# Row sums over partitions taken once per attention head, and once for the embedding, in place of once per half of the tokens

## The chip, the cores and the metric

The kernel runs on one core of a Trainium2 chip. The metric is device time in microseconds of one execution. A core has five engines that run their own instruction streams and wait for one another by semaphores: TensorE (PE, its weight loads shown apart as PEld), VectorE (DVE), ScalarE (ACT), GpSimd (POOL) and SyncE (SP), which here issues the DMAs. Line numbers, as L116, are those of the kernel before, unless the text says they are of the change.

## The reference

One layer of a hybrid encoder on 1024 tokens of width 1024. The normalised input goes through one projection of eight parts. Four parts feed differential attention (4 heads, two softmax maps each, an RMS norm per head and token, a gate), four a gated short convolution. Both are projected back together, normalised and added to x; an embedding p, projected and normalised per token, is added through a gate.

```python
h = rms_norm(x, pre_norm_gain[i])
proj = h @ w_in[i]
q, k, v, z_a, b_gate, c_gate, u, z_c = jnp.split(proj, N_IN_PARTS, axis=-1)
...
attn = diff_attention(q, k, v, lam, slopes)
attn = rms_norm(attn, subln_gain[i], SUBLN_EPS) * (1.0 - lambda_init)
attn = attn.reshape(bsz, seq, D_ATTN) * jax.nn.silu(z_a)
...
mixed = jnp.concatenate([attn, conv_out], axis=-1) @ w_out[i]
x = x + rms_norm(mixed, post_norm_gain[i])
e = rms_norm(p[i] @ w_ple_proj[i], ple_norm_gain[i])
x = x + jax.nn.sigmoid(x @ w_ple_gate[i]) * e
```

The change concerns two of these norms: the one of each head (`subln_gain`) and the one of the embedding (`ple_norm_gain`). Each needs, for every token, a sum of squares over features.

## The kernel before

Everything is held with features on the 128 partitions and tokens along the free axis, in two halves of 512 tokens (`HALF`). Products run in fp32 split into a high and a low part, so each tile product is three matmuls (`mm3`, L99 to L102) for each of eight slices of the contraction: 24 matmuls of 128x512 for one output tile of one half.

The program first projects the embedding (results go to `e_dram`), loads and scales x, and makes queries, keys and the values of all heads. Then come the four heads. Head h takes the projections of its query and key, and then the steps of its row of `PLAN` (L31 to L36): `a` is the softmax of four blocks of 128 queries (L220 to L254), `v` recalls the values, `z` projects the gate (`ev_z`, L214: the product by R, ACT's tanh at L217, the gate product L218), `g0` and `g1` are the value products of the two halves (`values`, L256), `n0` and `n1` apply the row scales (`scale_values`, L283), `c1` is one tile of the convolution's projections (L433 and around), and `s0`, `s1` are the sums of the embedding's two halves (`embed_scale`, L447). After the heads come the output projection, its norm and the gate.

A sum of squares per token is a sum over partitions. `column_sums` (L105) does it in four steps: DVE transposes 32x32 blocks (L107) and reduces over the 32 (L109), which leaves 128x16; an extra 16 columns (L111) carry a second quantity of the head, the inverse of its softmax sums; and a matmul with the constant matrix `fold` (L116) adds up the four groups of partitions. Its result lies in a PSUM bank of tag "t". There are two such banks, and the transposes of the attention weights (`tpw`, L264) go through the same two; a bank is given out again once the last reader of its former content is done.

In `values` the sum is followed by the row scale: DVE copies the extra columns (`rb`, L276), multiplies twice (L277 reads the bank, L278), scales (L96), POOL raises to the power -1/2 (`pow`, L97, with the constants of `nhalf`), DVE multiplies once more (L280). `scale_values` spreads the result over partitions by a transpose (L120 by L286) and multiplies it into the tile (L287). `embed_scale` reloads eight tiles of `e_dram`, squares them on ACT (L453), adds them on POOL (L455), and makes sum, pow and a factor 0.5 (L456 to L458).

Weight tiles are loaded and split by `load_w` (L122): ACT writes the high part (L89), POOL the low part `w` (L90). The attention weights `wt` are split by ACT (L89) and DVE (L90) after the transposes.

The order in which each engine works is not that of the source line by line. A scheduler places every engine's instructions at build time, by the steps of `PLAN`, the priorities that follow from them and its own model; each engine then runs its list strictly in order. Two or three steps are therefore interleaved: projections of one head fill PE while the softmax of another is under way.

```python
def bank_t(name):
    return ps_s.tile([P, HALF], F32, tag="t", bufs=2, name=name)
...
ms = bank_t("ms")
T.matmul(out=ms[:, :n], lhsT=fold, rhs=part[:, :n], start=True, stop=True)
```

## Time and profile before

| | |
|---|---|
| runs | 642.95, 643.99, 644.54 us; median 643.99 |
| the profiled execution | 643.39 us, of which the span of instructions is 641.6 and 1.8 lies outside |
| mean granted clock of TensorE | 0.996 of full speed |
| busy | PE 632.6 us (99%), DVE 447.9 (70%), ACT 242.3 (38%), POOL 227.6 (35%) |
| HBM | 48.4 MB read, 12.6 MB written, 95 GB/s over the span |

The profile is one execution. The bracket behind a row of a timeline says how long the engine stood idle before that instruction, and what released it. PE's instructions overlap, so the time that one costs is read from start to start. A wait is put down to the last of the semaphores that the instruction waited for.

### The profile page before, as it was taken

How to read it: one execution, taken by the hardware profiler on the slowest of the kernel's cores; microseconds unless marked ns; L12 is line 12 of the kernel's file. 1: busy time of each engine (PE TensorE's matmuls, PEld its weight loads, DVE VectorE, ACT ScalarE, POOL GpSimd, SP SyncE). 2: the span in 40 equal slices, each digit the busy share in tenths (PEclk: the TensorE clock that was granted, in tenths of full speed). 3: DMA queues.
4: the chain of work that ended last, by engine and by line, in shares of the span. 5: the costliest groups of instructions: out<-in, count | busy, mean ns of one | idle time of the engine just before them, and what ended most of it. 6: DMA issues, size and time to landing. Idle time of an engine off the chain costs nothing.

```text
span 641.6 us, 8064 instructions
## 1 busy us (share of the span) xinstructions
PE 632.6 (99%) x2941; PEld 524.8 (82%) x2941; DVE 447.9 (70%) x824; ACT 242.3 (38%) x442; POOL 227.6 (35%) x114
## 2 busy tenths in 40 slices
PE   8999999999999999999999999999999999999997
PEld 4888788888888888887888888888888888888886
DVE  6977612688786688776886999628993179898342
ACT  5936312334454333553343533322732225413111
POOL 2013300324326636237461142433760087741000
PEclk8999999999999999999999999999999999999999
DMA  8976612210244112353113411111360034124231
GB/s 301 391 268 161 228 78 102 88 39 27 83 130 149 50 33 59 85 170 97 36 33 90 127 46 34 42 55 36 119 242 33 2 98 150 64 84 146 84 114 50
DMA packets 35511, 67.78 MB, mean 106 GB/s; under 512 B 3600, under 2 KB 12304, under 8 KB 35472
## 3 DMA queue, kind: packets, MB, share of 16 engines
q1 hardware_dynamic: 35328, 67.14, 31.6%
q8 instruction: 23, 0.38, 0.2%
q10 hardware_dynamic: 144, 0.13, 0.1%
q14 instruction: 16, 0.13, 0.1%
HBM read 48.38 MB, written 12.58 MB: 95 GB/s over the span
## 4 chain that ended last, share of the span: by engine, by line
PE 89%; DVE 4%; DMA 3%; POOL 2%; ACT 1%; issue 1%; POOLq 0%; DVEq 0%; ACTq 0%
PE pj L100 13%; PE pj L102 13%; PE pj L101 13%; PE o L102 9%; PE o L100 9%; PE o L101 9%; PE s L237 5%; PE tpw L264 2%; PE v L100 2%; PE v L102 2%; PE v L101 2%; PE av L102 1%; PE ple L101 1%; PE av L101 1%; POOL mix L455 1%; PE av L100 1%
## 5 line engine op out<-in xcount | busy, mean ns | idle before, releaser
L100 PE MATMUL pj<-hT,w 128*128 128x512 f32 x448 | 176.3, 394 | 0.0
L101 PE MATMUL pj<-hT,w 128*128 128x512 f32 x448 | 176.2, 393 | 0.0
L102 PE MATMUL pj<-hT,w 128*128 128x512 f32 x448 | 176.2, 393 | 0.0
L90 POOL TENSOR_TENSOR w<-raw,w 128x1024 fp32r<-128x1024 f32 x41 | 105.6, 2581 | 145.1 <-ACT w L89 145.1
L102 PEld LDWEIGHTS pj<-hT,w 128*128 128x128 f32 x448 | 84.2, 188 | 16.4
L101 PEld LDWEIGHTS pj<-hT,w 128*128 128x128 f32 x448 | 84.2, 188 | 16.2
L100 PEld LDWEIGHTS pj<-hT,w 128*128 128x128 f32 x448 | 84.2, 188 | 16.1
L245 ACT ACTIVATE p<-p,nm 128x128 f32<-128x128 f32 (+7 forms) x64 | 49.4, 772 | 70.6 <-DVE nm L241 60.7
L89 ACT CAST w<-raw 128x1024 fp32r<-128x1024 f32 x44 | 45.8, 1047 | 19.4 <-issue 11.0
L102 PE MATMUL o<-x,w 128*128 128x512 f32 (+1 forms) x136 | 51.3, 377 | 0.0
L100 PE MATMUL o<-x,w 128*128 128x512 f32 (+1 forms) x136 | 51.2, 377 | 0.0
L101 PE MATMUL o<-x,w 128*128 128x512 f32 (+1 forms) x136 | 51.2, 377 | 0.0
L100 PE MATMUL o<-mT,w 128*128 128x512 f32 x128 | 49.8, 389 | 0.0
L101 PE MATMUL o<-mT,w 128*128 128x512 f32 x128 | 49.8, 389 | 0.0
L102 PE MATMUL o<-mT,w 128*128 128x512 f32 x128 | 49.7, 390 | 0.0
L237 PE MATMUL s<-ks,qs 128*128 128x512 f32 (+2 forms) x192 | 47.5, 346 | 0.5 <-ACT w L89 0.5
L89 ACT CAST wt<-tpw 128x512 fp32r<-128x512 f32 (+3 forms) x48 | 21.1, 479 | 60.2 <-PE tpw L264 60.2
L90 DVE TENSOR_TENSOR wt<-tpw,wt 128x512 fp32r<-128x512 f32 (+3 forms) x48 | 25.3, 550 | 26.3 <-ACT wt L89 26.2
L241 DVE CUSTOM_DVE_ANT_0 p<-s,bias 128x512 f32<-128x512 f32 (+3 forms) x64 | 34.8, 564 | 9.4 <-PE s L237 5.4
L237 PEld LDWEIGHTS s<-ks,qs 128*128 128x128 f32 x192 | 33.3, 188 | 5.8 <-ACT w L89 0.8
L418 POOL TENSOR_TENSOR mix<-mix,R 128x512 f32<-128x512 f32 x8 | 12.3, 1542 | 66.1 <-DVE mix L417 64.0
L253 DVE SCALAR_TENSOR_TENSOR p<-p,rl,p 128x128 f32<-128x128 f32 (+7 forms) x32 | 32.7, 1021 | 0.4
(142 smaller groups left out, 1101.6 us busy)
## 6 DMA issues: line engine op xcount, KB each, us to landing
raw<-in_w_in SPq DMA_DIRECT2D x32, 512.0 KB, 3.4
mix<-in_xT SPq DMA_DIRECT2D x16, 256.0 KB, 5.5
e_dram<-e SPq DMA_DIRECT2D x16, 256.0 KB, 6.0
mix<-e_dram SPq DMA_DIRECT2D x16, 256.0 KB, 3.0
ks<-ks SPq DMA_DIRECT2D x16, 256.0 KB, 3.6
v_dram<-v SPq DMA_DIRECT2D x8, 512.0 KB, 2.6
vs<-v_dram SPq DMA_DIRECT2D x32, 128.0 KB, 2.7
raw<-in_w_out SPq DMA_DIRECT2D x8, 512.0 KB, 3.3
```

Source lines behind the costliest of these rows:

```text
L89: A.copy(out=hi, in_=src)
L90: (lo_eng or V).tensor_tensor(out=lo, in0=src, in1=hi.bitcast(F32), op=sub)
L100: T.matmul(out=ps, lhsT=ah, rhs=bh, start=first, stop=False)
L101: T.matmul(out=ps, lhsT=ah, rhs=bl, start=False, stop=False)
L102: T.matmul(out=ps, lhsT=al, rhs=bh, start=False, stop=last)
L237: T.matmul(out=banks[m][:, :nn], lhsT=s.qs[:, m, qi], rhs=s.ks[:, m, part, c], start=part == 0, stop=part == 1)
L241: V.tensor_tensor_reduce(out=pr[m][:, c0:c0 + n], in0=banks[m][:, :n], in1=s.bias[:, b0:b0 + n], scale=-1.0, scalar=low[m], op0=add, op1=A ...
L245: A.activation(out=pr[m][:, :W], in_=pr[m][:, :W], func=AF.Exp, scale=-1.0, bias=low[m], accum_out=l[:, m:m + 1])
L253: V.scalar_tensor_tensor(out=pr[0][:, :W], in0=pr[1][:, :W], scalar=rl, in1=pr[0][:, :W], op0=mult, op1=add)
L264: T.transpose(out=tp[:, ii * P:(ii + 1) * P], in_=s.ws[ii][:, j * P:(j + 1) * P], identity=ident)
L418: G.tensor_tensor(out=o, in0=o, in1=R[n], op=mult)
L455: G.tensor_tensor(out=acc, in0=acc, in1=e, op=add)
```

## The change

The sum over partitions is cut in two functions. `partial` makes the reduction of one half into a given slice; `total` runs the matmul with `fold` over whatever width it is handed. In a head, `g0` and `g1` now only leave their reductions and extra columns in one tile of 64 columns (`part4`), and a new step `r`, `row_scales`, placed in `PLAN` after `g1` and a `c1` and ahead of `n0`, does one sum of 64 columns, then the products, the pow and the last product over 32 columns for both halves (lines 285 to 289 of the change, with L96 and L97 for the scale and the pow). The embedding's first half, in head 0, only leaves its reduction in `rs_e`; the second half, in head 1, does one sum, one pow and one factor 0.5 of 32 columns. The sums of x's norm and of the norm behind the output projection stay one per half; some small tiles are made wider so that addresses stay aligned, and `nhalf` has 32 columns.

The steps of `PLAN` change as shown for one head; the other three rows are changed in the same manner (`r` in all, `s` in the first two).

```
-    ['a0123', 'z', 'v', 'g0', 'a4567', 'g1', 'c1', 'n0', 'c1', 's1', 'n1', 'c1'],
+    ['a0123', 'z', 'v', 'g0', 'a4567', 'g1', 'c1', 'r', 'n0', 'c1', 's', 'n1', 'c1'],
```

```diff
-    small_c = edge.tile([P, 96], F32, name="small_c")
+    small_c = edge.tile([P, 224], F32, name="small_c")
...
-    nhalf = small_c[:, 4:20]
+    nhalf = small_c[:, 93:125]
...
-    def column_sums(acc, pool, extra=None, tag="flip"):
+    def partial(part, acc, pool, tag="flip"):
         flip = pool.tile([P, HALF], F32, tag=tag, name="flip")
         V.transpose(out=flip, in_=acc)
-        part = tiny.tile([P, 32], F32, tag="part", name="part")
-        V.tensor_reduce(out=part[:, 0:16], in_=flip.rearrange("p (f r) -> p f r", r=32), axis=AX.X, op=add)
-        if extra is not None:
-            V.tensor_tensor(out=part[:, 16:32].rearrange("p (t f) -> p t f", t=4),
-                            in0=extra.unsqueeze(2).broadcast_to([P, 4, 4]),
-                            in1=own.unsqueeze(1).broadcast_to([P, 4, 4]), op=mult)
-        n = 16 if extra is None else 32
-        ms = bank_t("ms")
-        T.matmul(out=ms[:, :n], lhsT=fold, rhs=part[:, :n], start=True, stop=True)
+        V.tensor_reduce(out=part, in_=flip.rearrange("p (f r) -> p f r", r=32), axis=AX.X, op=add)
+
+    def total(part):
+        ms = bank_t("ms")[:, :part.shape[-1]]
+        T.matmul(out=ms, lhsT=fold, rhs=part, start=True, stop=True)
         return ms
+
+    def column_sums(acc, pool, tag="flip"):
+        part = tiny.tile([P, 16], F32, tag="part", name="part")
+        partial(part, acc, pool, tag)
+        return total(part)
...
-    r_col = const.tile([P, NT + 80], F32, name="r_col")[:, :NT]
+    r_col = const.tile([P, NT + 96], F32, name="r_col")[:, :NT]
...
-                s.rs = {}
...
-                ms = column_sums(sq, ap, extra=r0)
-                rb = tiny.tile([P, 16], F32, tag="rb", name="rb")
-                rs = tiny.tile([P, 16], F32, tag="rs", name="rs")
-                V.tensor_copy(out=rb, in_=ms[:, 16:32])
-                V.tensor_tensor(out=rs, in0=ms[:, 0:16], in1=rb, op=mult)
+                if g == 0:
+                    s.part = tiny.tile([P, 64], F32, tag="part4", name="part4")
+                c = slice(16 * g, 16 * g + 16)
+                partial(s.part[:, c], sq, ap)
+                V.tensor_tensor(out=s.part[:, 32 + 16 * g:48 + 16 * g].rearrange("p (t f) -> p t f", t=4),
+                                in0=r0.unsqueeze(2).broadcast_to([P, 4, 4]),
+                                in1=own.unsqueeze(1).broadcast_to([P, 4, 4]), op=mult)
+
+            def row_scales(s):
+                ms = total(s.part)
+                rb = tiny.tile([P, 32], F32, tag="rb", name="rb")
+                rs = tiny.tile([P, 32], F32, tag="rs", name="rs")
+                V.tensor_copy(out=rb, in_=ms[:, 32:64])
+                V.tensor_tensor(out=rs, in0=ms[:, 0:32], in1=rb, op=mult)
                 V.tensor_tensor(out=rs, in0=rs, in1=rb, op=mult)
                 rsqrt(rs, rs, P, 1e-5)
                 V.tensor_tensor(out=rs, in0=rs, in1=rb, op=mult)
-                s.rs[g] = rs
+                s.rs = [rs[:, 0:16], rs[:, 16:32]]
...
-                r = tiny.tile([P, 16], F32, tag="rs", name="rsx")
-                rsqrt(r, column_sums(sums_x(n), rowp, tag="t")[:, :16], D, 1e-6)
+                r = tiny.tile([P, 32], F32, tag="rs", name="rsx")[:, :16]
+                rsqrt(r, column_sums(sums_x(n), rowp, tag="t"), D, 1e-6)
...
-            r = rs_e[:, 16 * n:16 * n + 16]
-            rsqrt(r, column_sums(acc, ap)[:, :16], D, 1e-6)
-            V.tensor_scalar(out=r, in0=r, scalar1=0.5, scalar2=None, op0=mult)
+            partial(rs_e[:, 16 * n:16 * n + 16], acc, ap)
+            if n:
+                rsqrt(rs_e, total(rs_e), D, 1e-6)
+                V.tensor_scalar(out=rs_e, in0=rs_e, scalar1=0.5, scalar2=None, op0=mult)
...
+                elif k == "r":
+                    hd.row_scales()
                 elif k == "s":
                     with tc.issue_after(hd.last.ins):
-                        embed_scale(int(v))
+                        embed_scale(h)
...
-            r = tiny.tile([P, 16], F32, tag="rs", name="rso")
-            rsqrt(r, column_sums(accs[n], cp)[:, :16], D, 1e-6)
+            r = tiny.tile([P, 32], F32, tag="rs", name="rso")[:, :16]
+            rsqrt(r, column_sums(accs[n], cp), D, 1e-6)
```

What each engine runs, and in which order, moves with it. Three places follow, as the two kernels' programs have them.

PE, head 0's sum. Before, at the sum of the second half (`ms`, and `pj` a projection, `s` scores of head 1):

```order
L237 MATMUL s_1919<-ks,qs 128x256 x2
L102 MATMUL pj<-hT_0_94,w 128x512
L116 MATMUL ms<-part,fold 128x32
L100 MATMUL pj<-hT_1_95,w 128x512
L101 MATMUL pj<-hT_1_95,w 128x512
```

In the change, at the one sum of the head, and further on, at the first transposes (`tpw`) behind it that need its bank:

```order
L102 MATMUL pj<-hT_0_94,w 128x512
L112 MATMUL ms<-part_1092,fold 128x64
L264 MATMUL tpw<-ident,p_1686 128x128
L264 MATMUL tpw<-ident,p_1706 128x128
L264 MATMUL tpw<-ident,p_1725 128x128
```

```order
L237 MATMUL s_1912<-ks,qs 128x512 x2
L100 MATMUL pj<-hT_7_101,w 128x512
L101 MATMUL pj<-hT_7_101,w 128x512
L264 MATMUL tpw<-ident,p_1706 128x128
L264 MATMUL tpw<-ident,p_1725 128x128
L100 MATMUL av<-wt,vs 128x512
L264 MATMUL tpw<-ident,p_1744 128x128
L237 MATMUL s_1913<-ks,qs 128x512 x2
L101 MATMUL av<-wt,vs 128x512
L102 MATMUL av<-wt,vs 128x512
```

The transposes of head 1's weights now stand right behind the sum. Four of them fill the other "t" bank; 28 instructions behind the sum's own end, the next transposes come back to the sum's bank.

DVE at the same place, from the product of the gate of head 1 (L216) on. Before:

```order
L216 TENSOR_TENSOR mix_1_113<-pj,R_129 128x512
L241 ISA p_1910,nm<-s_1912,bias 128x384
L241 ISA nm 128x1
L276 COPY rb<-ms 128x16
L277 TENSOR_TENSOR rs<-ms,rb 128x16
L218 SCALAR_TENSOR_TENSOR mix_1_113<-tz,mix_1_113 128x512
L278 TENSOR_TENSOR rs<-rs,rb 128x16
L96 TENSOR_SCALAR rs<-rs 128x16
L241 ISA p_1910,nm<-s_1920,bias,nm 128x256
```

In the change:

```order
L216 TENSOR_TENSOR mix_1_113<-pj,R_129 128x512
L241 ISA p_1883,nm<-s_1885,bias 128x384
L241 ISA nm 128x1
L285 COPY rb<-ms 128x32
L241 ISA p_1882,nm<-s_1884,bias 128x384
L241 ISA nm 128x1
L218 SCALAR_TENSOR_TENSOR mix_1_113<-tz,mix_1_113 128x512
L286 TENSOR_TENSOR rs<-ms,rb 128x32
L241 ISA p_1882,nm<-s_1892,bias,nm 128x256
L241 ISA nm 128x1
L287 TENSOR_TENSOR rs<-rs,rb 128x32
L96 TENSOR_SCALAR rs<-rs 128x32
```

The product that reads the sum's bank last (`rs<-ms,rb`) stood ahead of the gate product L218 and stands behind it now, and a split of `wt` and more score reductions (L241) stand behind that.

PE at the embedding's second sum. Before, and then in the change:

```order
L100 MATMUL pj<-hT_3_105,w 128x512
L101 MATMUL pj<-hT_3_105,w 128x512
L116 MATMUL ms<-part,fold 128x16
L264 MATMUL tpw<-ident,p_2491 128x128
```

```order
L102 MATMUL pj<-hT_0_94,w 128x512
L100 MATMUL pj<-hT_1_95,w 128x512
L112 MATMUL ms<-small_c,fold 128x32
L264 MATMUL tpw<-ident,p_2462 128x128
```

The sum went from between the projections of one weight tile to the next one's: between it and the last value product of head 1 there are 103 projection matmuls and 14 of the scores before, and 121 and 24 in the change.

## Rows read from the trace of the kernel before

**Rows 1.** The page's part 1, busy us (share) xinstructions of each engine

```profile
PE 632.6 (99%) x2941; PEld 524.8 (82%) x2941; DVE 447.9 (70%) x824; ACT 242.3 (38%) x442; POOL 227.6 (35%) x114
```

**Rows 2.** Stretches: length, busy of PE, PEld, DVE, ACT, POOL; clock, DMA, GB/s

```profile
200.00:300.00 100.00, 100.00 (x481) 83.84 (x480) 73.07 (x162) 42.63 (x81) 52.94 (x29) 1.00 0.28 85
300.00:305.00 5.00, 4.51 (x23) 3.54 (x23) 4.96 (x7) 0.59 (x1) 2.21 (x1) 1.00 0.33 104
305.00:475.00 170.00, 170.00 (x814) 141.98 (x814) 135.12 (x272) 66.26 (x121) 68.49 (x30) 1.00 0.24 78
```

**Rows 3.** What PE waited for: us in total, times, longest

```profile
PE ms L116 <- DVE part L109: 0.5, 1, 0.5
```

**Rows 4.** PE's timeline at head 0's two sums: start, us, instruction [idle <-releaser]

```profile
150.74 0.30 PE L116 MATMUL ms<-part,fold 128*128 128x32 f32 x2
150.88 0.41 PE L264 MATMUL tpw<-ident,p 128*128 128x128 f32 x2
151.05 0.48 PE L102 MATMUL pj<-hT,w 128*128 128x512 f32 x1
...
198.27 0.30 PE L116 MATMUL ms<-part,fold 128*128 128x32 f32 x2
```

**Rows 5.** PE's timeline at the second embedding sum

```profile
301.62 0.39 PE L100 MATMUL pj<-hT,w 128*128 128x512 f32 x1
...
302.53 0.39 PE L101 MATMUL pj<-hT,w 128*128 128x512 f32 x1
303.41 0.40 PE L116 MATMUL ms<-part,fold 128*128 128x16 f32 x2 [0.49 <-DVE part L109]
```

**Rows 6.** The chain of waits, 275 to 310 us: start, us, what

```profile
277.29 0.48 ACT sq L270
...
290.92 2.91 POOL rs L97
...
300.61 2.15 DVE ty L440
302.76 0.61 DVE part L109
```

**Rows 7.** DVE's timeline, 198.5 to 208 us

```profile
198.82 0.17 DVE L277 TENSOR_TENSOR rs<-ms,rb 128x16 f32<-128x16 f32 x1
201.63 2.84 DVE L218 SCALAR_TENSOR_TENSOR mix<-tz,mix 128x512 f32<-128x512 f32 x1 [2.64 <-ACT tz L217]
204.40 0.16 DVE L278 TENSOR_TENSOR rs<-rs,rb 128x16 f32<-128x16 f32 x1
```

**Rows 8.** ACT's timeline, 199 to 206 us

```profile
200.97 0.62 ACT L217 ACTIVATE tz<-mix 128x512 f32<-128x512 f32 x1
...
204.08 0.63 ACT L453 ACTIVATE mix<-mix 128x512 f32<-128x512 f32 x1 [1.07 <-DMA mix<-e_dram]
```

**Rows 9.** POOL's timeline, 198 to 214 us

```profile
201.53 2.39 POOL L90 TENSOR_TENSOR w<-raw,w 128x1024 fp32r<-128x1024 f32 x1
204.85 2.94 POOL L97 TENSOR_TENSOR rs<-rs,small_c 128x16 f32<-128x16 f32 x1 [0.92 <-DVE rs L96]
```

**Rows 10.** Groups of POOL by shape: count | busy, mean ns | idle before

```profile
L97 POOL TENSOR_TENSOR rs<-rs,small_c 128x16 f32<-128x16 f32 x8 | 23.7, 2961 | 16.6 <-DVE rs L96 16.5
...
L455 POOL TENSOR_TENSOR mix<-mix,mix 128x512 f32<-128x512 f32 x14 | 19.1, 1362 | 28.1 <-ACT mix L453 27.8
...
L77 POOL MEMSET small_c<- 128x16 f32 x1 | 0.1, 111 | 0.0
```

**Rows 11.** What DVE waited for

```profile
DVE rs L280 <- POOL rs L97: 6.2, 4, 2.4
```

**Rows 12.** Groups of DVE by shape

```profile
L90 DVE TENSOR_TENSOR wt<-tpw,wt 128x512 fp32r<-128x512 f32 x24 | 15.9, 683 | 21.3 <-ACT wt L89 21.1
...
L241 DVE CUSTOM_DVE_ANT_0 p<-s,bias,nm 128x256 f32<-128x256 f32 x16 | 7.6, 478 | 0.9 <-PE s L237 0.8
```

**Rows 13.** DVE's timeline, 290.9 to 293.9 us

```profile
292.19 0.69 DVE L440 SCALAR_TENSOR_TENSOR ty<-ty,y 128x512 f32<-128x512 f32 x1 [0.36 <-ACT ty L438]
```

6 rows, old and new, of the table PLAN are left out of this document.

## The prediction

> **What bounds the kernel now.** I read first the page's busy shares, then the table by stretches, then the waits of PE, then the timelines at the places that the change touches, and last the groups of POOL and DVE. Busy shares: PE works 632.6 us of the span, DVE 70%, POOL 35% [rows 1], so the time is PE's work plus the few moments in which PE stands. By stretches: PE is busy for the whole of 200 to 300 and of 305 to 475 us at full granted clock, and loses 0.49 us in the five microseconds between [rows 2]. PE's instruction order under the change differs from the order before only between about 147 and 473 us of the trace, so nothing outside that stretch can be won. The waits of PE name a single one in it: a row-sum matmul that waits 0.5 us for DVE's reduction [rows 3]. All that the change takes from DVE and POOL can therefore only matter where PE comes to wait for it.
>
> **The sums on PE.** A sum is two PE instructions. Start to start, the pair takes 150.88 - 150.74 = 0.14 us [rows 4]; nothing hides them, since PE is the bound. The change has 9 sums where there were 14, so 5 x 0.14 = 0.70 us go. Four of those left get 32 columns more, the one of the embedding 16 more. Lower bound of that: nothing. Upper bound: the rate of a wide matmul, 0.227 us for 512 columns (four of them from 301.62 to 302.53 [rows 5]), which is 0.014 us for 32 columns and, two instructions each, 4 x 0.028 + 0.014 = 0.13 us. I take the middle, 0.06. Sum: -0.64 us (-0.70 to -0.57).
>
> **The wait at 303 us.** The second embedding sum starts 303.41 - 302.53 = 0.88 us after the matmul ahead of it where 0.23 is usual [rows 5]: 0.65 us. The chain shows its cause: from the end of head 1's last product (the square at 277.29) through eight reloads, squares and POOL adds to the reduction at 302.76 there are about 26.1 us, one pow of 2.91 us on POOL among them, and a DVE product at 300.61 that took 2.15 us [rows 6]. Between head 1's last value product and this sum PE had 103 projection matmuls and 14 score matmuls, 58,400 columns or 25.8 us; in the order of the change it has 121 and 24, 70,208 columns or 31.1 us. If the pow there becomes twice as long, the chain grows by 2.9 to 29.0 us, still below 31.1. So I take the whole 0.65 us as gained; it stays if other work on POOL is put ahead of the chain. Term: -0.65 us (-0.65 to 0).
>
> **A new wait at 204 us.** Head 0's sum now stands at the place of its second half's sum, 198.1 us (198.27 less one pair [rows 4]). Its result lies in one of the two banks that the transposes of the weights use too. The next four transposes take the other bank; the ones behind them need this one. By the order of the change there lie between: the pair (0.14), four transposes (0.085 each, two in 151.05 - 150.88 [rows 4]), 22 matmuls of 512 columns (4.99) and two of 256 (0.23), so 5.7 us; PE wants the bank at 203.85 us. DVE frees it with its second reader, `rs<-ms,rb`. Before, that ran at 198.82, ahead of the gate product L218; now it stands behind L218. L218 started at 201.63, after 2.64 us of waiting for ACT's tanh, took 2.84 us, and L278 behind it ran at 204.40 [rows 7]; the tanh itself ran at 200.97 on ACT [rows 8]. L218 was that long because POOL split a weight tile from 201.53 for 2.39 us [rows 9]; the like product at 292.19 took 0.69 [rows 13].
>
> So the bank comes free at about 204.4 + 0.17 = 204.6, and PE stands 0.75 us. Behind it DVE still has a score reduction (0.48 and 0.08), L287, L96 (0.17 each, as L277 [rows 7]) and then the weight remainder (0.68 [rows 12]) that the second matmul of the value product needs, about 0.95 us of PE work after the late transpose, at 205.55. DVE is through at 206.05 to 206.1: another 0.5 us. A POOL add behind the square of 204.08 [rows 8] would hold L287 if two-input products are held by adds too, to about 206.05, and the remainder to 206.9: 1.3 instead of 0.5. Bounds: 0, if the weight split no longer falls on L218 (it then ends at 202.3), and 2.1. I take 1.3, since the split, the tanh and L218 stand in the same neighbourhood in both orders.
>
> By the Trainium skill, "SBUF — State Buffer", section Terms, a port pair shared by VectorE and GpSimd is locked for the full instruction and "the loser **fully blocks**"; its contention section includes VectorE operations with two inputs in SBUF. The trace agrees at 201.63, with 2.84 us, and does not agree for the pow, beside which a product took 0.69 us. By the rule alone the new wait would be 2.1 us and the sum +0.8.
>
> **The wider pows.** The head's and the embedding's pows go from ten of 16 columns to five of 32. The price of 32 is in no row. Lower bound: 2.96 us, if columns cost nothing; upper: 5.9, if it is per column. A memset of the same 16 columns took 0.11 us and an add of 512 columns 1.36 [rows 10], so little of 2.96 is fixed, and I take 5.9. POOL's total is then unchanged, and its idle time of 65% [rows 1] takes it. DVE needs the result for the last scale product, L289. The DVE work that the order of the change has between L96 and L289 is, by the groups' means, about 6.5, 5.3, 4.8 and 4.1 us in heads 0 to 3; the shortest is six products of 128x512 at 0.68 [rows 12]. DVE then waits about 0, 0.6, 1.1 and 1.8 us. Before, it waited four times at this place, 2.4 us at the longest [rows 11], and PE waited for none of it [rows 3]. Cost: nothing (0 to 3.5). If that cover went, a late weight remainder or a late transposed bank would be next to hold PE.
>
> **The rest.** Some 22 small DVE operations go, about 0.17 us each [rows 7], 3.7 us of an engine with 30% to spare: nothing, and what they free on DVE is idle time. The embedding's first half no longer asks PE for a sum in head 0, and the factor 0.5 is applied once. DMAs and ACT's instructions are the same in number. The row scales of head 3's first half come later: from their sum to the output projection's first use of that tile the order has about 22 us of PE work, and the pow with the products ahead of and behind it is some 12 by the groups' means: nothing.
>
> **Sum.** -0.64 - 0.65 + 1.3 = 0.0 us. On the profiled execution that is 643.4 us; the median of the three runs lies 0.6 above it (643.99; the runs reach from 642.95 to 644.54), and the forecast on it is 644.0.
>
> **Rivals.** 0.3%, 1.93 us, is about what a measurement of this kernel can tell from no change.
> - *The new wait costs nothing* (0.25). The scheduler's order and the real times part: if the weight split on POOL lands a microsecond or two away, L218 takes 0.7 us and the bank is free before 203.85. Then -1.3 us: 642.7. For it: these 2 us decide all. Against: nothing in the change moves that split. Runs that scatter like those shown put some of this case beyond 0.3%.
> - *The wait at 303 us remains* (0.13). The longer pow or another split ahead of the adds eats the 2.1 us between 29.0 and 31.1. Then 644.6.
> - *Slower: the doubled pow reaches PE* (0.14). DVE runs in order; with L289 waiting, the remainders and reductions behind it wait as well. It decides from the point where the wait exceeds what the place can bear, 2.4 us by [rows 11] in the order before, perhaps less in the new one. With all of 0.6 + 1.1 + 1.8 = 3.5 us on PE: 647.5. For it: four bursts instead of eight are less evenly spread. Against: the longest wait forecast, 1.8, is below 2.4.
> - *Slower: the pow holds DVE as the weight split does* (0.03). Then nothing covers it: each head's DVE stands up to 5.9 us, 3.5 above what was borne, 14 us in four heads: 658. Against it stands the product of 0.69 us at 292.19 [rows 13], inside the pow at 290.92 [rows 6]. This is what the page named above would have, if a pow counts as its GpSimd operation that reads SBUF.
> - That the change does not do what it says is left out: the order has 9 sums and 5 pows fewer.
>
> **How the numbers follow.** The likeliest case, no measurable change at 644.0, has 0.45. Faster by over 0.3% is 0.10, all of it out of the 0.25 at 642.7. Slower is 0.14 + 0.03 = 0.17. The remaining 0.73 lies within 0.3%. The range goes from 642.1, the case at 642.7 with the scatter of the runs, to 646.3, the last rival with two thirds of its price; it leaves out some 0.1 on each side.
>
> **What would show it.** PE with 10 instructions fewer, sums of 64 columns at 0.14 to 0.17 us; no wait of a sum near 303 us; a wait of a transpose on `rs`, and of a value product on `wt`, near 204 us, 1.3 us together; pows of 5.9 us with DVE waits below 2. Wrong it would be with PE idle above 3 us between 147 and 473 us, or with pows of 32 columns near 3 us, or with none of the waits at 204.

## The result and the profile after

| | before | after |
|---|---|---|
| median | 643.47 us (642.71 to 644.67, 6 runs) | 648.99 us (648.06 to 655.21, 6 runs) |
| ratio of the means | | 1.011, 95% interval 1.0087 to 1.0133 |
| the profiled execution | 643.39 us, span 641.6 | 648.06 us, span 645.8 |

The changed kernel is slower, by 5.5 us (0.9%) between the medians and by 1.1% between the means, where no change was forecast (644.0, range 642.1 to 646.3). Two of its six runs took 652.9 and 655.2 us, at a mean granted clock of 0.991 and 0.990, and raise the mean; the other four lie within 1 us of one another at 0.996 or more, and why those two are longer is not shown, since there is no trace of them.

The page's part 1, the table of what PE waited for and the stretches (length, busy of PE, PEld, DVE, ACT and POOL; clock, DMA share, GB/s) answer to [rows 1], [rows 3] and [rows 2]:

```profile
PE 633.0 (98%) x2931; PEld 523.2 (81%) x2931; DVE 441.4 (68%) x802; ACT 242.3 (38%) x442; POOL 223.9 (35%) x109
```

```profile
PE o L100 <- DVE mix L454: 2.5, 1, 2.5
...
PE s L237 <- issue: 1.6, 1, 1.6
...
PE tpw L264 <- DVE rs L286: 0.6, 1, 0.6
PE av L101 <- DVE wt L90: 0.6, 1, 0.6
```

```profile
200.00:300.00 100.00, 97.06 (x462) 80.05 (x460) 73.38 (x161) 41.26 (x80) 53.44 (x27) 1.00 0.30 85
...
475.00:625.00 150.00, 147.57 (x653) 122.27 (x654) 97.25 (x102) 42.78 (x71) 54.84 (x26) 1.00 0.28 96
```

DVE has 22 instructions less and PE 10, as the order had it. But PE, which lost 0.5 us between 150 and 475 us before [rows 2, 3], now loses 2.94 in 200 to 300 and 2.43 behind 475 us. The wait of the embedding's sum is gone; four others and some smaller losses are there instead. The timeline of PE shows the four (start, duration, instruction, idle time before it and its releaser):

```profile
204.03 0.41 PE L264 MATMUL tpw<-ident,p 128*128 128x128 f32 x2 [0.61 <-DVE rs L286]
205.84 0.50 PE L101 MATMUL av<-wt,vs 128*128 128x512 f32 x1 [0.59 <-DVE wt L90]
...
290.91 0.39 PE L100 MATMUL pj<-hT,w 128*128 128x512 f32 x1
292.90 0.47 PE L237 MATMUL s<-ks,qs 128*128 128x256 f32 x2 [1.60 <-issue]
...
474.58 0.39 PE L102 MATMUL o<-mT,w 128*128 128x512 f32 x1
477.43 0.47 PE L100 MATMUL o<-mT,w 128*128 128x512 f32 x1 [2.46 <-DVE mix L454]
```

From start to start against the usual 0.227 us, the last two cost 1.77 (292.90 - 290.91 less 0.227) and 2.62 us (477.43 - 474.58 less 0.227), the first two 0.77 and 0.76; smaller ones at 285.4 and 410.4 us cost 0.31 and 0.16. The sums themselves did what was said; the pair of 64 columns takes 197.52 - 197.35 = 0.17 us:

```profile
197.35 0.33 PE L112 MATMUL ms<-part,fold 128*128 128x64 f32 x2
197.52 0.50 PE L264 MATMUL tpw<-ident,p 128*128 128x128 f32 x3
```

An instruction that both kernels run in the same place behind the heads, the first `rso` scaling, gives the balance. One line for each kernel, before and then after (first and last start behind the durations):

```profile
L96 DVE TENSOR_SCALAR rso<-ms x2: 167/170/173, 513.9 to 558.5; 128x16 f32<-128x16 f32 x2
```

```profile
L96 DVE TENSOR_SCALAR rso<-ms x2: 167/171/175, 518.5 to 563.1; 128x16 f32<-128x16 f32 x2
```

It starts 4.6 us later. The terms: 0.6 gained in the first 75 us, where the order is the same in both and arrivals differ from run to run; 0.6 gained by the sums; 0.65 by the embedding's sum [rows 5]; 1.53 lost at 204 us; 2.08 at 285 and 291 us; 2.78 at 410 and 475 us. Together 4.54 us.

**204 us.** DVE's timeline of after, beside [rows 7]:

```profile
200.94 2.85 DVE L218 SCALAR_TENSOR_TENSOR mix<-tz,mix 128x512 f32<-128x512 f32 x1 [2.54 <-ACT tz L217]
203.71 0.18 DVE L286 TENSOR_TENSOR rs<-ms,rb 128x32 f32<-128x32 f32 x1
...
204.21 0.77 DVE L287 TENSOR_TENSOR rs<-rs,rb 128x32 f32<-128x32 f32 x1
...
205.10 0.68 DVE L90 TENSOR_TENSOR wt<-tpw,wt 128x512 fp32r<-128x512 f32 x1
```

The gate product L218 again started beside a weight split of POOL (200.83 to 203.23) and took 2.85 us; the last reader of the sum's bank stood behind it, then the remainder of `wt`. L287, 0.18 us elsewhere, took 0.77: it stood until POOL's add of 203.19 to 204.92 ended, so adds hold such a product too. This is the wait that was forecast, 1.53 for 1.3 us.

**291 us.** One piece of the chain of waits of after, and the rows of POOL, ACT and DVE that follow it:

```profile
278.69 7.15 DMA mix<-e_dram
```

```profile
288.92 2.85 POOL L90 TENSOR_TENSOR w<-raw,w 128x1024 fp32r<-128x1024 f32 x1 [0.55 <-ACT w L89]
```

```profile
285.86 0.63 ACT L462 ACTIVATE mix<-mix 128x512 f32<-128x512 f32 x1 [5.57 <-DMA mix<-e_dram]
...
289.28 0.61 ACT L217 ACTIVATE tz<-mix 128x512 f32<-128x512 f32 x1
```

```profile
289.93 2.39 DVE L218 SCALAR_TENSOR_TENSOR mix<-tz,mix 128x512 f32<-128x512 f32 x1 [0.40 <-ACT tz L217]
292.24 0.55 DVE L241 CUSTOM_DVE_ANT_0 p<-s,bias 128x384 f32<-128x384 f32 x1
```

In the change head 1's value products end about 12 us earlier than before (the square behind them starts at 265.27, not at 277.29 [rows 6]), and with them the embedding's second half begins earlier, amid the reloads of values, the exchange of queries and keys and weight loads on the same DMA queue. A reload issued at 278.69 lands 7.15 us later; before, one took 2.7 to 2.9. Others in the crowd are late too: the weight loads of 262 to 294 us took 7.2 us to land in the median, 3.4 before. ACT runs in order and stands 5.57 us on that reload; two exponentials, a cast and another square later the tanh for head 2's gate runs at 289.28, so L218 starts at 289.93, within a weight split (288.92 to 291.77), and takes 2.39 us. The score reduction behind it ends at 292.80, and PE's scores start at 292.90. The profile names no releaser for that wait (`issue`); that the scores waited for the bank which this reduction reads is inferred from the two times.

**475 us.** The end of the heads, first POOL, ACT and DVE of the change, then POOL and DVE of before:

```profile
448.70 5.42 POOL L97 TENSOR_TENSOR rs<-rs,small_c 128x32 f32<-128x32 f32 x1 [0.34 <-DVE rs L96]
...
460.15 14.18 POOL L90 TENSOR_TENSOR w<-raw,w 128x1024 fp32r<-128x1024 f32 x5 [6.03 <-ACT w L89]
```

```profile
456.41 2.71 ACT L89 CAST mT<-mix 128x512 fp32r<-128x512 f32 x5 [5.50 <-DVE mix L296]
459.03 2.94 ACT L89 CAST w<-raw 128x1024 fp32r<-128x1024 f32 x3
```

```profile
466.38 2.88 DVE L449 SCALAR_TENSOR_TENSOR ty<-ty,y 128x512 f32<-128x512 f32 x1
...
472.00 2.88 DVE L450 SCALAR_TENSOR_TENSOR mix<-ty,mix 128x512 f32<-128x512 f32 x1
...
476.61 0.68 DVE L454 TENSOR_TENSOR mix<-pj,mix 128x512 f32<-128x512 f32 x1
```

```profile
455.36 8.05 POOL L90 TENSOR_TENSOR w<-raw,w 128x1024 fp32r<-128x1024 f32 x3 [3.25 <-ACT w L89]
463.78 5.24 POOL L90 TENSOR_TENSOR w<-raw,w 128x1024 fp32r<-128x1024 f32 x2 [0.37 <-ACT w L89]
```

```profile
471.90 0.68 DVE L445 TENSOR_TENSOR mix<-pj,mix 128x512 f32<-128x512 f32 x1
```

The pow of 32 columns ends at 454.12. Only then can either half of the last head's tile be scaled, where before the first half was scaled at 445 us. ACT's casts of `mT` wait for it at 456.41, and the casts of the output weights stand behind them; so POOL's five splits run from 460.15 to 474.33. Before, the same five ran from 455.36 to 469.02, and held DVE's products as much: what is new is that they come 4.8 us later, while PE by then is only 1.9 us later than before (the balance above without its last wait). DVE's products, on which the last convolution tile depends, run about one for each split, 2.9 us each. L454 comes at 476.61; the same product came at 471.90 before. PE waits 2.46 us for it.

### The profile page after: what moved, and what is told of

Same layout as the page of the kernel before. It is cut to its first block, busy times and chain, and to the rows that moved or that the text cites. A ratio compares the mean times of both kernels' runs of the same rounds, so it can differ in the third digit from the quotient of the medians.

```text
span 645.8 us, 8007 instructions
## 1 busy us (share of the span) xinstructions
PE 633.0 (98%) x2931; PEld 523.2 (81%) x2931; DVE 441.4 (68%) x802; ACT 242.3 (38%) x442; POOL 223.9 (35%) x109
## 4 chain that ended last, share of the span: by engine, by line
PE 79%; DVE 8%; DMA 5%; ACT 3%; issue 2%; SPq 1%; POOL 1%; DVEq 0%; POOLq 0%; ACTq 0%
PE pj L101 12%; PE pj L102 12%; PE pj L100 12%; PE o L100 9%; PE o L102 8%; PE o L101 8%; PE s L237 4%; DMA mix<-e_dram 3%; PE tpw L264 2%; PE v L100 2%; PE v L101 2%; PE v L102 2%; PE av L101 1%; DVE ql L90 1%; PE av L102 1%
## 5 line engine op out<-in xcount | busy, mean ns | idle before, releaser
L241 DVE CUSTOM_DVE_ANT_0 p<-s,bias 128x512 f32<-128x512 f32 (+3 forms) x64 | 34.7, 565 | 9.5 <-PE s L237 5.5
L427 POOL TENSOR_TENSOR mix<-mix,R 128x512 f32<-128x512 f32 x8 | 10.8, 1344 | 67.9 <-DVE mix L426 67.9
L585 ACT ACTIVATE tg<-o 128x512 f32<-128x512 f32 (+1 forms) x17 | 9.7, 572 | 57.3 <-PE o L102 53.5
```

The costliest lines, as they stand in the source:

```text
L241: V.tensor_tensor_reduce(out=pr[m][:, c0:c0 + n], in0=banks[m][:, :n], in1=s.bias[:, b0:b0 + n], scale=-1.0, scalar=low[m], op0=add, op1=A ...
L427: G.tensor_tensor(out=o, in0=o, in1=R[n], op=mult)
L585: A.activation(out=t, in_=ps, func=AF.Tanh, scale=0.5)
```

## The experiments

Theory 1: the change's loss is these waits, and each comes from where the merged steps put DVE's products and ACT's casts against POOL's weight splits and the embedding's reloads. Rivals: the doubled pow is the whole loss wherever it stands; one of the two merges costs and the other is free; or any new order of so full a program draws waits of the same sum. All runs are timed against the kernel before on the same chip; each is given as its median and the ratio of its mean to that of the kernel before, with the interval.

**One half of the change at a time.** heads_only takes the embedding's sums back to one per half; embed_only changes nothing but these.

```diff
-            partial(rs_e[:, 16 * n:16 * n + 16], acc, ap)
-            if n:
-                rsqrt(rs_e, total(rs_e), D, 1e-6)
...
+            r = rs_e[:, 16 * n:16 * n + 16]
+            rsqrt(r, column_sums(acc, ap), D, 1e-6)
```

> The change with the embedding's sums again half by half; the heads' stay merged. Theory 1 (the merged row scales of the heads put DVE products and ACT casts where POOL's weight splits hold them; waits near 204, 291 and 475 us): most of the loss stays, 3 to 5.5 us over the kernel before, with a PE wait of over 2 us at the start of the output projection. Rival (the merged embedding sum is what costs, through the reloads and adds): within 1 us of before.

> The kernel before with the embedding's sum alone merged. Theory 1: 0 to 1 us faster than before (the 0.65 us wait of the second embedding sum goes, and one PE pair of 0.14 us). Rival (the merged embedding sum costs): 2 us slower or more, with the wait of scores near 291 us that the change has.

heads_only: 646.67 us, 1.0051 (1.0034 to 1.0068). embed_only: 653.74 us, 1.0159 (1.0139 to 1.0178). Theory 1 held for the first in time (3.75 us between the medians), though of its three waits only the last is there; it missed on the second by 10 us: the smaller half of the change is the dearer one alone, and the two do not add up. What PE waited for in the two, heads_only first:

```profile
PE o L102 <- POOL w L90: 1.9, 1, 1.9
```

```profile
PE pj L100 <- DVE mix L445: 3.1, 1, 3.1
PE s L237 <- DVE nm L241: 2.0, 2, 1.0
...
PE tpw L264 <- DVE p L253: 1.5, 3, 0.9
```

heads_only has nothing to speak of in the heads, at 204 us neither, although L218 is held for 2.84 us there as well (201.29) and the last reader of the sum's bank starts at 204.06: its order has no transposes on PE at that place. It has 2.4 us at the start of the output projection, on weight casts and splits. embed_only, which takes one pair of 0.14 us from PE and half a chain from DVE, got another order on every engine, and with it six waits from 203 us on. The longest is for a convolution product behind DVE's splits of `mT` at the end of the heads (465.72 us), as in the change at 475 us, with every pow at 16 columns: a wait of that kind can come without the wide pow. DVE's timeline shows what two others follow:

```profile
201.82 2.84 DVE L218 SCALAR_TENSOR_TENSOR mix<-tz,mix 128x512 f32<-128x512 f32 x1 [2.55 <-ACT tz L217]
```

```profile
216.62 2.91 DVE L287 SCALAR_TENSOR_TENSOR mix<-flipa,small_c,mix 128x512 f32<-128x512 f32 x1
```

At 201.82 it is the same L218 beside the same split, with another reduction behind it; at 216.62 another product (L287) beside the split of 216.58.

**The last head by halves.** Step `r` goes from its row of the plan; `values` calls the row scale for each half:

```diff
+                if s.h in (3,):
+                    s.rs = (s.rs if g else []) + s.row_scales(c)
```

> The change with the last head's row scale again half by half; heads 0 to 2 and the embedding stay merged. Theory 1: the 2.7 us lost at 475 us go, since the casts of that head's tile on ACT no longer hold up the casts of the output weights: about 2.5 us faster than the change. Rival (that wait comes from the convolution's last tiles, whatever the row scale does): the wait of over 2 us at 475 us stays, time as the change.

649.97 us, 1.0097 (1.0069 to 1.0126). The wait at 475 us is gone (0.42 us at 465 us is left), as theory 1 had it; the time is not 2.5 us better, as it said, because the wait at 291 us was 3.61 us in its profile and the clock fell behind it. The stretch with that wait and the one behind it (the clock is the figure behind POOL):

```profile
289.00:294.20 5.20, 1.59 (x8) 1.00 (x7) 5.16 (x6) 0.63 (x1) 3.97 (x3) 0.87 0.31 101
294.20:299.50 5.30, 5.30 (x14) 4.24 (x15) 4.71 (x10) 1.55 (x3) 0.00 (x0) 0.50 0.01 2
```

From 294.2 to 299.5 us the granted clock is 0.50, the lower of the two levels (1.2 GHz), after PE had done 1.59 us of work in 5.2 us; 12 matmuls then take 0.2 us more each, 2.4 us on top of the wait.

**The weight splits in halves,** on the change and on the kernel before:

```diff
-            (lo_eng or V).tensor_tensor(out=lo, in0=src, in1=hi.bitcast(F32), op=sub)
+            if lo_eng is G:
+                for a in range(0, KT, 4):
+                    G.tensor_tensor(out=lo[:, a:a + 4], in0=src[:, a:a + 4], in1=hi[:, a:a + 4].bitcast(F32), op=sub)
+            else:
+                (lo_eng or V).tensor_tensor(out=lo, in0=src, in1=hi.bitcast(F32), op=sub)
```

> The change with each of POOL's weight splits (128x1024) made in two instructions of 128x512. Theory 1 (a DVE product that meets a split stands until that POOL instruction ends, and that is what made PE wait at 204, 291 and 475 us): the gate products at 201 and 290 us take at most 1.6 us where they took 2.85 and 2.39, the waits behind them fall by over half, and the time is 2 to 5 us below the change. Rival (the two engines share what they read from, so the product is slowed as long as there is splitting, however it is cut): products as long as before, time within 1 us of the change.

> The kernel before with the same cut of POOL's weight splits. Theory 1: its held products reach PE hardly anywhere (the wait of the sum at 303 us follows one, 0.65 us), so within 1 us of before, at most 0.7 faster. Rival (the cut itself is worth several us whatever the order): 2 us or more faster than before.

after_pieces2: 651.38 us, 1.0099 (1.0074 to 1.0123). before_pieces2: 641.67 us, 0.9962 (0.9950 to 0.9974). The order on PE is the same but for a few rows. DVE's row and POOL's rows of the cut change at 201 us:

```profile
201.16 1.73 DVE L222 SCALAR_TENSOR_TENSOR mix<-tz,mix 128x512 f32<-128x512 f32 x1 [2.29 <-ACT tz L221]
```

```profile
201.06 2.99 POOL L92 TENSOR_TENSOR w<-raw,w 128x512 fp32r<-128x512 f32 x2
204.01 1.28 POOL L468 TENSOR_TENSOR mix<-mix,mix 128x512 f32<-128x512 f32 x1
```

The product took 1.73 us where it took 2.85: it stands until the POOL instruction that runs ends, not until the splitting ends. That much of theory 1 holds. Its time did not follow: the wait at 204 us only fell from 1.53 to 1.2 us, since two small operations behind L218 were held in turn, one by the second piece of the split and one by an add of the embedding (204.01 to 205.29). At 291 us the tanh came just as late and PE lost 2.9 us and the clock, and at 481 us PE waits 2.99 us where it waited 2.46. On the kernel before, the sum at 303 us no longer waits, and the cut is worth 2.5 us: not theory 1's 0.7 at the most, but what the rival said. The profiled execution is 1.2 us shorter, of which that wait is 0.65; where the rest comes from is not shown. A second run beside another kernel, expected below, gave 641.75 us, 0.9975 (0.9961 to 0.9989), 2.1 us below before, so the gain is real.

> The kernel before with POOL's weight splits in two instructions, a second time, beside the one above: 2 to 3 us below before, as the first time (ratio 0.9962); if that was the chip's doing, within 1 us of before.

**Splits moved to DVE** for output weight tiles 1 to 3:

```diff
-                tiles[k] = load_w(src[m], pool=wp if k % KT in (1, 4, 7) else wp2)
+                tiles[k] = load_w(src[m], pool=wp if k % KT in (1, 4, 7) else wp2, lo_eng=V if k in (1, 2, 3) else G)
```

> The change with the low parts of output weight tiles 1 to 3 made by DVE (about 1.2 us each) instead of POOL. Theory 1 (the burst of five splits on POOL from 460 us holds the products ahead of the last convolution product, on which the output projection waits at 475 us): that wait of 2.6 us shrinks below 1 us, the waits at 204 and 291 us stay, time 1.5 to 2.7 us below the change. Rival (DVE is simply late there and gets more work by this): the wait grows by 1 to 3 us.

650.86 us, 1.0096 (1.0060 to 1.0131). The wait at 475 us is 2.4 us as in the change, neither smaller nor larger: ahead of L454 DVE did two splits at 1.2 us itself and met four of POOL's instead of five. This run tells nothing of the cause.

**A shorter pow:**

```diff
-                rsqrt(rs, rs, P, 1e-5)
+                V.tensor_scalar(out=rs, in0=rs, scalar1=1.0 / P, scalar2=1e-5, op0=mult, op1=add)
+                G.tensor_tensor(out=rs[:, 0:16], in0=rs[:, 0:16], in1=nhalf[:, 0:16], op=ALU.pow)
```

> The change with the heads' pow over the first 16 columns only; the second half of each head stays without its power of -1/2, so its output is left unnormalised. Theory 1 (place and order): the wait at 204 us stays, since it lies ahead of the pow; those at 291 and 475 us shrink by no more than the pow does (2.5 us each at the most): 1 to 4 us below the change. Rival 2 (the length of the pow is the whole cause): no PE wait above 0.5 us in the heads, time within 0.5 us of before or faster.

653.27 us, 1.0138 (1.0124 to 1.0152): slower than the change, against both. The scheduler gave another order (the embedding's sum now waits 3.9 us at 294 us). It tells only that a shorter operation does not make this kernel faster by itself.

**The embedding's second half in head 2,** alone and with the last head by halves, and this with the splits cut. In the plan `'s'` goes from head 1's row to head 2's, and

```diff
-                        embed_scale(h)
+                        embed_scale(min(h, 1))
```

> The change with the embedding's second half reloaded and summed in head 2 instead of head 1. Theory 1, as mended by the runs so far (at 291 us PE waits because ACT, which runs in order, stands 5.6 us on an embedding reload that lands 7.2 us after its issue, in a crowd of value reloads, weight loads and exchanges of keys; the softmax and the tanh behind it are late): no PE wait above 0.5 us between 270 and 300 us, those at 204 and 475 us as in the change, about 2 us below the change. Rival (the gate product held by POOL's split is enough by itself): a wait of over 1 us stays near 291 us.

> The change with both mended: the last head's row scale by halves and the embedding's second half in head 2. Theory 1: the waits at 291 and 475 us go, that at 204 us (1.3 to 1.5 us) stays: 0 to 1.5 us over the kernel before. Rival (any new order brings new waits of the same sum): 3 us or more over the kernel before, with waits at places not seen so far.

> The same with POOL's weight splits in two instructions each. Theory 1: the wait at 204 us shrinks too; 0 to 2 us below the kernel before, near the kernel before with the same cut (2.5 us below it). Rival: no better than without the cut, since cutting brought the change nothing (it stayed 6 us over).

659.52 us, 1.0249 (1.0228 to 1.0270); 652.19 us, 1.0152 (1.0124 to 1.0180); 653.40 us, 1.0151 (1.0133 to 1.0168). In s_late the wait at 291 us is gone and PE waits at 357, 364, 372 and 377 us instead, 0.7, 0.4, 0.6 and 4.0 us, and 3.35 us where the change waits at 475. The largest two:

```profile
376.94 0.80 PE L100 MATMUL pj<-hT,w 128*128 128x512 f32 x1 [4.00 <-DVE mix L426]
...
485.68 0.76 PE L100 MATMUL o<-mT,w 128*128 128x512 f32 x1 [3.35 <-DVE mix L454]
```

So the wait at 291 us went with the reloads, as theory 1 had it, and the time, forecast 2 us below the change, came out 10 us above it. The rival of the second run, new waits at new places with a new order, held in all three, and their sum was larger.

**The pow's length by itself.** First attempts, before_pow32 (`rs` of the kernel before made 32 columns wide, and the pow over all of them) and two_pows:

```diff
-                rsqrt(rs, rs, P, 1e-5)
-                V.tensor_tensor(out=rs, in0=rs, in1=rb, op=mult)
-                s.rs = [rs[:, 0:16], rs[:, 16:32]]
+                V.tensor_scalar(out=rs, in0=rs, scalar1=1.0 / P, scalar2=1e-5, op0=mult, op1=add)
+                s.rs = []
+                for g in range(2):
+                    c = slice(16 * g, 16 * g + 16)
+                    r = tiny.tile([P, 16], F32, tag=f"rs{g}", name=f"rs{g}")
+                    G.tensor_tensor(out=r, in0=rs[:, c], in1=nhalf[:, :16], op=ALU.pow)
+                    V.tensor_tensor(out=r, in0=r, in1=rb[:, c], op=mult)
+                    s.rs.append(r)
```

> The kernel before with every pow of a head done over 32 columns, 16 of them spare: eight pows of 5.4 us in place of 2.96, sums still half by half. Rival 2 (the longer pow alone is what costs): 3 us slower than before or more. Theory 1 (the place of the row scale counts, the pow only as part of its length): within 1.5 us of before.

> The change with each head's pow made in two instructions of 16 columns, the first half's first, each followed by its own last product. Theory 1 (in the last head both halves of the scaled tile come only after 5.4 us of pow, so DVE's scale products and splits all fall into POOL's burst of weight splits): the first half is scaled about 2.7 us sooner, and the wait at 475 us falls by 1.5 us or more; the waits at 204 and 291 us stay within 1 us. Rival (the burst is late for another reason, the order of ACT's casts): the wait at 475 us stays above 2 us.

648.49 us, 1.0081 (1.0066 to 1.0097), and 649.86 us, 1.0107 (1.0082 to 1.0131). Both edits also moved the tiles behind the small ones off multiples of 512 bytes, by 192 and 384 bytes, and PE's pace in quiet stretches was slower in these two alone. before_off192 shows that by itself, and the two were repeated with the tiles back in place:

```diff
-    r_col = const.tile([P, NT + 80], F32, name="r_col")[:, :NT]
+    r_col = const.tile([P, NT + 128], F32, name="r_col")[:, :NT]
```

> The kernel before, its order of instructions the same, with 48 spare columns more behind r_col, so that the tiles that follow begin 192 bytes past a multiple of 512. Theory (the place of a tile in SBUF sets how fast a matmul reads it): 231 to 234 ns between matmuls that read such tiles, 2 to 4 us slower than before. Rival (those two runs were disturbed): 227 ns and the time of before.

> The kernel before with pows of 32 columns, 16 of them spare, and its tiles on multiples of 512 bytes. Theory 1 (the pow's length alone costs what PE waits for at the start of the output projection): 1 to 3 us over before, all of it near 467 us. Rival 2 (the longer pow is the whole loss): 4 us or more over before.

> The change with each head's pow in two instructions of 16 columns, tiles on multiples of 512 bytes. Theory 1: the wait at 475 us is the pow's doing and is gone, those at 204 and 291 us stay: 2 to 3 us below the change, 2 to 3.5 us over before. Rival: as the change.

before_off192: 645.80 us, 1.0047 (1.0034 to 1.0060), with the order of before. PE's timeline of the value projections, before_off192 and then the kernel before:

```profile
80.13 0.40 PE L100 MATMUL v<-wv,hT 128*128 128x512 f32 x1
...
81.77 0.39 PE L101 MATMUL v<-wv,hT 128*128 128x512 f32 x1
```

```profile
80.17 0.39 PE L102 MATMUL v<-wv,hT 128*128 128x512 f32 x1
...
81.76 0.39 PE L100 MATMUL v<-wv,hT 128*128 128x512 f32 x1
```

Seven matmuls take 81.77 - 80.13 = 1.64 us in the one and 81.76 - 80.17 = 1.59 in the other, 0.234 and 0.227 each.

before_pow32_al: 645.93 us, 1.0037 (1.0024 to 1.0050). PE waits for nothing in the heads, and 1.15, 0.21, 0.22 and 0.25 us at 467 to 470 us for weight casts and splits:

```profile
467.00 0.50 PE L100 MATMUL o<-mT,w 128*128 128x512 f32 x1 [1.15 <-ACT w L89]
```

Behind them the granted clock is 0.50 from 470 to 472 us. The wider pow alone, on the kernel before, costs 2.6 us between the medians (2.4 by the ratio), all at the end of the heads and in part as clock. two_pows_al: 646.18 us, 1.0040 (1.0026 to 1.0055), 2.85 us over before where the change is 5.5 over. The same 5.8 us of POOL, but the first half's result after 2.9:

```profile
450.11 5.76 POOL L293 TENSOR_TENSOR rs<-rs,small_c 128x16 f32<-128x16 f32 x2 [0.34 <-DVE rs L288]
460.10 8.59 POOL L90 TENSOR_TENSOR w<-raw,w 128x1024 fp32r<-128x1024 f32 x3 [4.23 <-ACT w L89]
469.06 2.42 POOL L90 TENSOR_TENSOR w<-raw,w 128x1024 fp32r<-128x1024 f32 x1 [0.38 <-ACT w L89]
```

```profile
453.04 0.18 DVE L294 TENSOR_TENSOR rs<-rs,rb 128x16 f32<-128x16 f32 x1 [1.02 <-POOL rs L293]
...
473.76 0.68 DVE L459 TENSOR_TENSOR mix<-pj,mix 128x512 f32<-128x512 f32 x1
```

POOL's burst is three splits and one right behind, the last convolution product (here L459) runs at 473.76, and PE waits for nothing there. The burst begins no earlier than in the change (460.10 for 460.15): what the shorter first pow brought is one split less ahead of L459, in an order of ACT's casts that is another too, and this run does not part the two. The waits of the change at 204 and 291 us stay (0.4 and 0.6, and 1.4).

**Heads merged, pow in two, the embedding by halves,** and this with the splits cut:

> Heads' sums merged, the embedding's half by half, the heads' pow in two instructions of 16 columns. Theory 1: the 2.4 us that heads_only lost at 467 us shrink below 1 us, no wait above 0.7 us in the heads: from 1 us faster to 1 us slower than before. Rival (any new order draws new waits): 2 us or more over before.

> Heads' sums merged, pow in two instructions, the embedding by halves, POOL's weight splits in two instructions each. Theory 1: the 1.55 us at 466 us shrink below 0.5 us and the 0.55 us of four sums appear: 0.3 to 1 us below the kernel before with the same cut. Rival (any new order draws new waits): equal to that kernel or slower.

643.49 us, 1.0003 (0.9992 to 1.0015); with the cut 641.87 us, 0.9970 (0.9957 to 0.9983), beside 0.9975 for the kernel before with the cut. One wait of 1.4 us on a weight split stays at 468 us in the first, where below 1 us was expected, and of 1.3 in the second. So what four sums save is not seen; the rival of the second run, equal or slower, held.

Four of the runs differ in two things alone, the embedding's sums (merged or by halves) and the heads' pow (in one or in two). Their medians over that of the kernel before:

| | pow in one | pow in two |
|---|---|---|
| embedding merged | 5.5 us (the change) | 2.85 us (two_pows_al) |
| embedding by halves | 3.75 us (heads_only) | 0.16 us (heads_two_pows) |

Taking back the embedding's merge gains 1.8 and 2.7 us, cutting the pow gains 2.7 and 3.6, and with both the loss is gone, while the heads' sums stay merged; each figure is good to about 1 us. So neither the wider pow nor one of the merges is the whole loss. This holds for these four orders: embed_only, whose heads are those of before, has the embedding's merge at 10.8 us.

The kernel that beats both is the one before with the weight splits in halves; merging adds nothing to it.

## Why the prediction was wrong

**The sums on PE** (-0.64 us): the sizes were right, 0.13 to 0.17 us for a pair.

**The wait at 303 us** (-0.65): it went, as forecast, but the step asked only whether the embedding's chain is done in time for its own sum, and not whom that chain delays. Beginning earlier, it put a reload in a crowd on the DMA queue ahead of ACT's exponentials and tanh. It gave back 2.08 us at 285 and 291 us, so the step, with bounds of -0.65 to 0, came to about +1.4. That the embedding's reloads are in it is shown by s_late, where the wait went with them, and by heads_only and heads_two_pows, where none is there; in all three the rest of the order moved too.

**A new wait at 204 us** (+1.3): right in place, cause and size (1.53). That it came at all hangs on the whole order: heads_only has the same held product and no wait. By the Trainium skill, "SBUF — State Buffer", section Terms, the loser of the shared port pair blocks for the full instruction of the other; the cut splits agree (1.73 us for 2.85, until the running piece ended). For the pow the page's rule does not hold here: L218 at 280.32 took 0.69 us in the middle of a pow that ran from 277.98 to 283.43, as at [rows 13].

**The wider pows** ("cost: nothing"): this is the step that failed most, with 2.62 us at 475 us where nothing was forecast; the one at 303 us failed beside it. The price of 5.9 us was near (5.44 for the heads', 5.90 for the embedding's). The cover was counted only up to DVE's own wait at L289, which indeed stayed below 2 us (two waits, 1.92 and 1.74). What was not followed is what stands behind L289 in the last head: the scale products, ACT's casts of `mT`, behind them on ACT the casts of the output weights, and POOL's burst of splits, which then falls on DVE's products. before_pow32_al prices the length alone at 2.6 us, within the bounds of 0 to 3.5 that the step gave, not at the nothing that it took; the table of four runs prices it at 2.7 and 3.6 us. Two edits that bring the last head's first half earlier, head3_halves and two_pows_al, lose the wait at 475 us. The path from the pow to that wait, cast by cast, is read from one trace and argued only: embed_only has a like wait with pows of 16 columns, and in two_pows_al the splits begin no earlier.

**The rest** ("the row scales of head 3's first half come later: nothing"): the same failure from the other side. The slack of 22 us was that of PE's first use of the tile; the work that the delay pushed together was not added up engine by engine.

The rival "the doubled pow reaches PE" came nearest (647.5, chance 0.14). Its path was another: not DVE waiting at L289 in each head, but the crowd behind it in the last one. "The pow holds DVE" is refuted by L218 at 280.32, above. Why the embedding's merge alone gives the worst order is not settled either: the runs show the waits and what PE waited for, not why the scheduler's order came out that way.

## What to carry to other kernels

Where one engine is busy 98% of the time and a scheduler orders the rest, an edit that saves half a microsecond is worth what the new order's waits leave of it: forecast the widest waits of every engine that runs in order behind the moved step (ACT's casts and reloads too), not only the step's own. Joining two small chains into one costs latency: both results come when the longer one is done, and what waited for the first now crowds with what waited for the second; what it saved here, 0.14 us a sum, is seen in no run's time. Cutting a long instruction of the engine that holds another's reads shortens each such meeting (1.73 us for 2.85). It gave 2.1 and 2.5 us on the kernel before and nothing on the change, so it has to be tried in the order that it will run in.

## What the runs showed of the hardware that was not expected

- A wait of PE can cost clock as well, and the length of the one wait does not tell whether it will. Behind waits of 2.73 to 4.00 us (after_pieces2, head3_halves, h3_s_late, s_late) the granted clock was 0.50 for 2 to 6 us; behind the change's own waits of 1.60 and 2.46 us it stayed at 1.00; but in before_pow32_al it fell to 0.50 behind four waits within 4 us, of which the longest was 1.15 us and the sum 1.83.
- Tiles that begin 192 bytes past a multiple of 512 slowed the matmuls that read them from 0.227 to 0.234 us and the kernel by 0.47%, with the order of instructions unchanged; which boundary counts was not tried. The padding in the change's `r_col` line keeps its tiles in place, and two experiments were spoilt by leaving it as it was.
